# Layer 1 of a hybrid encoder: memory heads placed among the state-space units, the units' states in PSUM, and a wider filler rule for VectorE

## The chip, the core and the metric

The kernel runs on one core of a Trainium2 chip. The core has TensorE (PE: matmuls, with weight loads shown as PEld), VectorE (DVE), ScalarE (ACT), GpSimd (POOL) and SyncE (SP, which here issues every DMA). SBUF is the working memory, PSUM the eight banks of 512 float32 words a partition into which matmuls write; POOL works on SBUF alone here. The metric is the device time of one execution in microseconds (us).

## The reference, cut to what matters

Two post-norm layers over 512 tokens of width 1024, one batch. Layer 0 has a convolution branch, latent attention with 8 heads and attention of 4 heads into 256 memory tokens. Layer 1 has a bidirectional S5 state-space branch and another 4-head memory attention:

```python
def odd_layer(x, mem, w_in, s5_fwd, s5_bwd, s5_d, w_glu, w_mem_kv, w_out, ln_g, ln_b):
    h = x @ w_in
    s5_u, s5_gate, mem_q, mem_gate = _split(h, ODD_SPLITS)
    y = s5_direction(u, *s5_fwd, reverse=False) + s5_direction(u, *s5_bwd, reverse=True)
    y = y.reshape(bsz, seq, S5_DIM) + s5_d * s5_u
    z = jax.nn.gelu(y) @ w_glu
    c_out = (z[..., :S5_DIM] * jax.nn.sigmoid(z[..., S5_DIM:])) * jax.nn.silu(s5_gate)
    m_out = memory_attention(mem_q, mem, w_mem_kv) * jax.nn.silu(mem_gate)
    out = jnp.concatenate([c_out, m_out], axis=-1) @ w_out
    return layer_norm(ALPHA * x + out, ln_g, ln_b)
```

The memory heads need only `h` and the memory tokens; the state-space branch does not feed them. The gated products (`z @ w_glu`) need all 1024 channels of `z`, so every state-space unit must be done first.

## The kernel before

Every float32 product is made of three products of a rounded part and a remainder (`mm3`). So each weight that arrives by DMA is first copied to its rounded part by ScalarE (a CAST) and then has its remainder taken by VectorE (a TENSOR_TENSOR), both 128x1024; a projection of 128 output channels is then 24 matmuls of 512 columns. The loads go through `wload`; up to three raw weights are held.

The code does not issue instructions as it is written. It records them (`Prog.record`), and `Prog.schedule` then places all of them in one list by a simulation of its own with costs per instruction: an instruction is placed when its inputs are ready, its engine is free and its tiles can be had. SBUF and PSUM space is given out by tag; `QUOTA` says how many tiles of a tag may live at once. Instructions are taken by their recorded order (`prio`), up to a `WINDOW` of 500 recorded instructions ahead; background work (convolution taps, the state-space tables of `s5_prep`) fills gaps. Each engine then runs its part of that list in order, and waits by semaphores. The scheduler marks instructions with `port`: those of POOL, and those of VectorE that read two SBUF tensors. It takes them to exclude each other, and when VectorE would find the port taken it looks for one of its instructions that needs no port and ends soon enough (line 432).

Layer 1 is `layer1`. After the memory keys and values (`mem_kv`) come eight input projections `s5_u`, then eight units `s5_unit(i)`, each with the projection of one gate (`gate`) behind it, then the four memory heads (`mem_attn`), then eight gated products (`glu_out`, two projections each) and the output projection (`out_proj`), whose order is memory heads first.

A unit holds 128 channels. TensorE makes the input of the states (8 products of 256 columns, line 1314), transposes it (8 transposes, line 1325) into two PSUM banks Z, its real and imaginary part. VectorE then rotates by a table E: four products E*Z; two additions give Vr. Four scans of 64 partitions (forward on 64, backward on the others, for each part) give W, whose first or last column in each of 8 groups is then set to zero. Four products E*W and two additions give X, the states. TensorE multiplies X and the inputs with tables C and strips (24 products, line 1367), and after every second unit the result is transposed (line 1380), goes through GELU on ScalarE and becomes two of the eight z tiles. Seven loads of a unit come from tables that `s5_prep` wrote to device memory in layer 0.

A memory head is one gate projection, one projection of queries, scores in two banks (12 matmuls of 256 columns), a softmax with exponentials on ScalarE, 8 transposes and 6 matmuls with the values.

Of the kernel before, what the change touches and what calls it, by code (L numbers as in the profile page):

```python
# [14 lines left out]
F32 = mybir.dt.float32  # L15
# [3 lines left out]
ALU = mybir.AluOpType  # L19
# [4 lines left out]
P = 128  # L24
# [37 lines left out]

SB_WORDS = {"S": 21504, "R": 26624, "Z": 4864}
ENGINES = ("PE", "DVE", "ACT", "POOL", "SP")
QUOTA = dict(wr=3, wh=4, wl=4, wrv=1, whv=1, wlv=1, wrk=1, whk=1, wlk=1, A=4, S=3, T=2, R=1, Q=1, O=4, V=1, Z=2, W=2, Y=1, pr=6, bb=2, bt=2, nat=2, ncim=2, strips=2, qE=1, qt=2, qbt=1, qpw=1, qC=2, qB=1, C=2, D=1, cgl=2)
INF = float("inf")
NEAR, RESERVE = 30, dict(R=3584, S=2048)
RESERVEP = dict(R=4096, S=2560)
RESERVE1 = dict(R=2048, S=512)
WINDOW = dict(PE=500, DVE=500, ACT=700, POOL=500, SP=250)  # L70
# [109 lines left out]
class Prog:  # L180
# [108 lines left out]
    def schedule(self):  # L289
# [26 lines left out]
        order, left, t = [], len(self.ops), 0.0  # L316
# [86 lines left out]
        while left:  # L403
# [12 lines left out]
            t, e = max(t, best[0]), best[1]  # L416
# [7 lines left out]
            while pend[e] and pend[e][0][0] <= t:  # L424
                r, p, i, o = heapq.heappop(pend[e])
                heapq.heappush(avail[e], (p, i, o))
            skipped, got = [], None
            near = main[front].prio + NEAR if front < len(main) else INF
            if e == "DVE" and port > t + 80.0:

                for c in sorted(avail[e])[:40]:
                    if not c[2].port and c[2].cost < port - t + 150.0 and (c[2].bg or c[0] <= near - NEAR + WINDOW[e]) and alloc(c[2], near):
                        got = c[2]
                        avail[e].remove(c)
                        heapq.heapify(avail[e])
                        break
            while got is None and avail[e] and len(skipped) < 200:
                if not avail[e][0][2].bg and front < len(main) and avail[e][0][0] > main[front].prio + WINDOW[e]:

                    c = next((x for x in sorted(avail[e]) if x[2].bg), None)  # L440
# [4 lines left out]
                else:  # L445
                    c = heapq.heappop(avail[e])
# [91 lines left out]
class Kernel:  # L538
# [132 lines left out]
    def setup(self):  # L671
        nc, A = self.nc, self.A
        self.ident = self.ct([P, P], F32, "ident")
        self.ones = self.ct([P, P], F32, "ones")
        self.mhalf = self.ct([P, 8], F32, "mhalf")
        self.halfpi = self.ct([P, 1], F32, "halfpi")
        self.vec = self.ct([P, V_TOT], F32, "vec")
        nc.vector.memset(self.ones[:], 1.0)
        self.ones_r = self.ct([P, P], F32R, "onesr")
        nc.scalar.copy(self.ones_r[:], self.ones[:])  # L680
        nc.vector.memset(self.mhalf[:], -0.5)
        nc.vector.memset(self.halfpi[:], 1.5707963267948966)

        warm = self.bank("Y")
        for _ in range(8):
            nc.tensor.matmul(warm[:, 0:P], lhsT=self.ones[:], rhs=self.ones[:], start=True, stop=True)

        self.X = []

        W = [[nc.tile([P, 1024], dt, tag) for dt, tag in ((F32, "wr"), (F32R, "wh"), (F32R, "wl"))] for _ in range(2)]  # L690
        for step in ((0, 0, 256), 0, 1, (1, 0, 256), (0, 256, 1024), 2, 3, (1, 256, 1024), 4, 5, 6, 7):
            if isinstance(step, int):
                raw = self.big()
                nc.sync.dma_start(out=raw[:], in_=A["xT"][step // 2][:, (step % 2) * N:(step % 2 + 1) * N])
                self.X.append(self.split(raw[:]))
            else:
                c, sl = step[0], slice(*step[1:])
                raw, hi, lo = (t[:, sl] for t in W[c])
                nc.sync.dma_start(out=raw, in_=A["w1"][c][:, sl])
                self.split_into(raw, hi, lo)  # L700
        self.w0 = [w[1:] for w in W]
# [280 lines left out]
        V = [self.split(ps[:]) for ps in pv]  # L982
        return K, V

    def mem_attn(self, wq, wg, act, K, V):
        nc = self.nc
        scale = 128.0 ** -0.5
        out = []
        for h in range(4):
            g = self.gate(wg[h], act)  # L990
            ps = self.projF(wq[h], act, 8)
            qh, ql = self.split(ps[:])
            kh, kl = (x[:, (h % 2) * 256:(h % 2) * 256 + 256] for x in K[h // 2])
            pr = []
            for u in range(2):
                s = self.bank("S")
                for i in range(2):
                    t = 2 * u + i
                    self.mm3(s[:, i * 256:i * 256 + 256], [(qh[:, t * P:(t + 1) * P], ql[:, t * P:(t + 1) * P])],
                             [(kh, kl)])  # L1000
                mx = self.sm(2, tag="mx2")
                nc.vector.reduce_max(mx[:], s[:].rearrange("p (a b) -> p a b", a=2), axis=AX.X)
                p = self.big(F32, "pr")
                for i in range(2):
                    sl = slice(i * 256, i * 256 + 256)
                    self.softmax_tail(s[:, sl], p[:, sl], scale, mx[:, i:i + 1])
                pr.append(p)
            pt = []
            for m in range(2):
                tp = self.bank("T")  # L1010
                for t in range(4):
                    c = (t % 2) * 256 + m * P
                    nc.tensor.transpose(tp[:, t * P:(t + 1) * P], pr[t // 2][:, c:c + P], self.ident[:])
                pt.append(self.split(tp[:]))
            o = self.bank("V")
            vs = slice(h * P, h * P + P)
            self.mm3(o[:], [(v[0][:, vs], v[1][:, vs]) for v in V], [(a[:], b[:]) for a, b in pt])
            nc.vector.scalar_tensor_tensor(g[:], o[:], 0.5, g[:], op0=ALU.mult, op1=ALU.mult)
            out.append(g)
        return out  # L1020


    def out_proj(self, wname, mix, resid, grow, brow, finish, tail):
# [269 lines left out]
    def s5_unit(self, i):  # L1293
# [34 lines left out]
        nc.scalar.copy(dv, self.m8[:, i * 8:i * 8 + 8].unsqueeze(2).to_broadcast([P, 8, 64]))  # L1328
        G.memset(dv[0:64, :, 0:1], 0.0)
        G.memset(dv[64:128, :, 63:64], 0.0)  # L1330
        Vr = [self.big(), self.big()]
        t = [self.tmp() for _ in range(2)]
        V.tensor_tensor(Vr[0][:], E[0], Z[0][:], op=ALU.mult)
        V.tensor_tensor(t[0][:], E[1], Z[1][:], op=ALU.mult)
        V.tensor_tensor(Vr[1][:], E[0], Z[1][:], op=ALU.mult)
        V.tensor_tensor(t[1][:], E[1], Z[0][:], op=ALU.mult)
        G.tensor_tensor(Vr[0][:], Vr[0][:], t[0][:], op=ALU.add)
        G.tensor_tensor(Vr[1][:], Vr[1][:], t[1][:], op=ALU.subtract)
        W = [self.big(), self.big()]
        for x in range(2):  # L1340
            wv = W[x][:].rearrange("p (n k) -> p n k", n=8)
            V.tensor_tensor_scan(W[x][0:64, 1:N], D0[0:64, 0:N - 1], Vr[x][0:64, 0:N - 1], 0.0,
                                 op0=ALU.mult, op1=ALU.add)
            V.tensor_tensor_scan(W[x][64:128, 0:N - 1][:, ::-1], D0[64:128, 1:N][:, ::-1],
                                 Vr[x][64:128, 1:N][:, ::-1], 0.0, op0=ALU.mult, op1=ALU.add)
            G.memset(wv[0:64, :, 0:1], 0.0)
            G.memset(wv[64:128, :, 63:64], 0.0)
        X = [self.big(), self.big()]
        t = [self.tmp() for _ in range(2)]
        G.tensor_tensor(X[0][:], E[0], W[0][:], op=ALU.mult)  # L1350
        V.tensor_tensor(t[0][:], E[1], W[1][:], op=ALU.mult)
        G.tensor_tensor(X[1][:], E[0], W[1][:], op=ALU.mult)
        V.tensor_tensor(t[1][:], E[1], W[0][:], op=ALU.mult)
        G.tensor_tensor(X[0][:], X[0][:], t[0][:], op=ALU.subtract)
        G.tensor_tensor(X[1][:], X[1][:], t[1][:], op=ALU.add)
# [5 lines left out]
        for q in range(4):  # L1361
            c = q * P
# [67 lines left out]
    def layer0(self):  # L1430
# [11 lines left out]
        K, V = self.mem_kv("m0")  # L1442
        mq = A["w1"][40:44]
        mgt = A["w1"][44:48]
        mem = self.mem_attn(mq, mgt, self.xact, K, V)
        for c in range(4):
            nc.sync.dma_start(out=self.mixd[8 + c][:], in_=mem[c][:])
        self.rope_tables()
# [48 lines left out]
    def layer1(self):  # L1497
        nc, A = self.nc, self.A
        nc.res = RESERVE1
        act = lambda k: tuple(x[:, k % 4] for x in self.H[k // 4])  # L1500
        K, V = self.mem_kv("m1")
        self.z, self.sg = [None] * 8, [None] * 8
        for i in range(8):
            self.s5_u(i, act)
        for i in range(8):
            self.s5_unit(i)
            self.sg[i] = self.gate(A["w2"][8 + i], act)
        mem = self.mem_attn(A["w2"][16:20], A["w2"][20:24], act, K, V)
        mem = [self.split(m[:]) for m in mem]
        zact = lambda k: (self.z[k][0][:], self.z[k][1][:])  # L1510
        cs = [self.glu_out(c, zact) for c in range(8)]
        grow, brow = self.rows("o_ln_g", "o_ln_b")
        ov = self.out.rearrange("(k s) d -> s k d", s=SC)

        def finish(t, h):

            for half in range(2):
                for s in range(2):
                    nc.sync.dma_start(out=ov[2 * t + s, :, half * N:(half + 1) * N], in_=h[half][s * NCH:(s + 1) * NCH, :])

        def resid(t, half):
            r = self.tmp()
            nc.sync.dma_start(out=r[:], in_=self.h1d[t][half][:])
            return r

        self.out_proj("wo1", mem + cs, resid, grow, brow, finish, TAIL[1])
# [94 lines left out]
```

## Time and profile before

| | us |
|---|---|
| median of 3 runs | 1098.17 |
| lowest and highest | 1095.62, 1101.28 |
| profiled execution, its time | 1099.12 |
| its span, first to last instruction | 1097.3 |
| PE busy | 1016.5 (93%) |
| DVE busy | 805.2 (73%) |
| ACT busy | 440.9 (40%) |
| POOL busy | 558.5 (51%) |
| mean granted TensorE clock | 0.966 |

A share over the whole span is a mean over stages with different limits, so the stages are read one by one: the windows below give each engine's busy time in a stretch, the chain of waits says what each piece of the path waited for, and the groups by form give how long one instruction takes. All instructions carry one line number (535, where the list is emitted), so groups are told apart by engine, operation and tiles: `sb` and `sr` are the SBUF arenas, `sz` the one for small tiles, `ps` is PSUM, `scr` device memory, `w` the layers' input weights.

### The profile page before, as it was taken

The numbers are of one execution on the slowest core, as the hardware profiler recorded it, in microseconds if no ns is written. First come the engines' busy times: TensorE is split into PE (matmuls) and PEld (weight loads), VectorE is DVE, ScalarE is ACT, GpSimd is POOL, SyncE is SP. The second block draws the span as 40 slices with busy tenths as digits, with TensorE's granted clock in tenths as the row PEclk, the third lists the DMA queues.
The fourth block names the chain that finished last, engine by engine and source line by source line (L and its number), as shares of the span: only waits on it lengthen the run. The fifth ranks groups of instructions, "written<-read, shape, count | busy, mean of one in ns | idle before, by whom it ended". The sixth has DMA issues, their size and how long they took to land.

```text
span 1097.3 us, 15060 instructions
## 1 busy us (share of the span) xinstructions
PE 1016.5 (93%) x5296; PEld 797.7 (73%) x5296; DVE 805.2 (73%) x1252; ACT 440.9 (40%) x760; POOL 558.5 (51%) x805
## 2 busy tenths in 40 slices
PE   9999899999999979996889899997788799999996
PEld 7888678878777646764667688875556588888885
DVE  6787999999899888889885448419677946543346
ACT  5433356364323554566562224422222356422210
POOL 0554568758799687895989901006556600000001
PEclk9999999999999988998999899999899899999998
DMA  7434534335775262546396754984676422333413
GB/s 252 138 113 146 162 107 162 135 106 181 248 231 178 65 209 96 169 129 212 127 306 211 272 186 146 304 285 122 195 221 222 118 77 78 114 135 120 147 60 76
DMA packets 80171, 180.02 MB, mean 164 GB/s; under 512 B 24160, under 2 KB 28896, under 8 KB 80096
## 3 DMA queue, kind: packets, MB, share of 16 engines
q1 hardware_dynamic: 80096, 179.07, 50.2%
q8 instruction: 41, 0.67, 0.3%
q14 instruction: 34, 0.28, 0.1%
HBM read 142.93 MB, written 36.11 MB: 163 GB/s over the span
## 4 chain that ended last, share of the span: by engine, by line
PE 53%; DVE 11%; DMA 8%; POOL 7%; ACT 4%; issue 2%; SPq 1%; DVEq 0%; ACTq 0%; POOLq 0%
PE ps L535 53%; POOL sb L535 7%; DVE sr L535 4%; DMA sb<-w 4%; DVE ps L535 4%; DVE sb L535 2%; ACT sb L535 2%; ACT sr L535 2%; DMA scr<-sb 1%; DMA sb<-wo 1%; SPq L535 1%; DMA sb<-pos 1%; DVE sz L535 0%; DMA sb<-m1v 0%; POOL sz L535 0%
## 5 line engine op out<-in xcount | busy, mean ns | idle before, releaser
L535 PE MATMUL ps<-sr 128*128 128x512 f32 (+2 forms) x3904 | 933.4, 394 | 55.7 <-ACT sr L535 38.7
L535 PEld LDWEIGHTS ps<-sr 128*128 128x128 f32 (+1 forms) x3904 | 715.8, 192 | 229.8 <-ACT sr L535 45.2
L535 DVE TENSOR_TENSOR sr<-sb,sr 128x1024 fp32r<-128x1024 f32 (+4 forms) x230 | 274.4, 1203 | 165.6 <-ACT sr L535 142.1
L535 POOL TENSOR_TENSOR sb<-sb 128x512 f32<-128x512 f32 (+6 forms) x278 | 297.6, 1084 | 110.5 <-DVE sb L535 59.4
L535 ACT CAST sr<-sb 128x1024 fp32r<-128x1024 f32 (+4 forms) x230 | 201.1, 887 | 334.6 <-PE ps L535 180.8
L535 POOL TENSOR_TENSOR sz<-sz 128x64 f32<-128x64 f32 (+2 forms) x75 | 41.4, 556 | 252.9 <-DVE sz L535 252.8
L535 DVE SCALAR_TENSOR_TENSOR ps<-sb,sz,ps 128x505 f32<-128x505 f32 (+14 forms) x240 | 168.6, 736 | 0.3
L535 POOL TENSOR_TENSOR sb<-sb,sz 128x512 f32<-128x512 f32 (+4 forms) x160 | 132.3, 845 | 29.2 <-DVE sz L535 10.7
L535 ACT COPY sb<-ps 128x512 f32<-128x512 f32 (+3 forms) x78 | 41.0, 541 | 95.6 <-PE ps L535 74.2
L535 DVE SCALAR_TENSOR_TENSOR sb<-sb,ps 128x512 f32<-128x512 f32 x64 | 47.4, 740 | 42.1 <-ACT sb L535 22.9
L535 ACT CAST sr<-ps 128x512 fp32r<-128x512 f32 (+1 forms) x100 | 55.4, 571 | 52.7 <-PE ps L535 52.1
L535 DVE TENSOR_TENSOR sr<-ps,sr 128x512 fp32r<-128x512 f32 (+1 forms) x100 | 65.1, 661 | 12.4 <-ACT sr L535 10.2
L535 PE MATMUL ps<-sz,sb 128*128 128x128 f32 (+2 forms) x608 | 63.6, 238 | 8.7 <-ACT sb L535 5.6
L535 PEld LDWEIGHTS ps<-sz,sb 128*128 128x128 f32 (+1 forms) x608 | 46.9, 131 | 28.4 <-ACT sb L535 14.8
L535 PE MATMUL ps<-sb 128*64 128x128 f32 (+2 forms) x768 | 56.9, 302 | 6.2 <-POOL sb L535 2.4
L535 POOL TENSOR_TENSOR sb<-sz 64x64 f32<-64x64 f32 (+1 forms) x128 | 58.9, 469 | 4.8
L535 ACT ACTIVATE sb<-ps 128x512 f32<-128x512 f32 (+1 forms) x72 | 38.1, 548 | 51.2 <-PE ps L535 37.2
L535 PEld LDWEIGHTS ps<-sb 128*64 128x64 f32 (+1 forms) x768 | 35.6, 129 | 30.9 <-issue 18.8
L535 POOL MEMSET sb<- 64x8 f32 (+2 forms) x80 | 11.0, 148 | 89.0 <-DMA scr<-sb 34.8
L535 DVE TENSOR_TENSOR_SCAN sb<-sb 64x511 f32<-64x511 f32 x32 | 50.2, 1570 | 6.8 <-POOL sb L535 2.5
L535 ACT ACTIVATE sb<-ps,sz 128x256 f32<-128x256 f32 (+1 forms) x64 | 36.6, 578 | 36.4 <-DVE sz L535 31.3
L535 DVE TENSOR_REDUCE sz<-ps 128x1 f32<-128x512 f32 (+1 forms) x48 | 32.0, 684 | 14.2 <-PE ps L535 14.0
(45 smaller groups left out, 350.4 us busy)
## 6 DMA issues: line engine op xcount, KB each, us to landing
sb<-w SPq DMA_DIRECT2D x70, 512.0 KB
sb<-scr SPq DMA_DIRECT2D x48, 512.0 KB
scr<-sb SPq DMA_DIRECT2D x40, 512.0 KB
sb<-scr SPq DMA_DIRECT2D x76, 256.0 KB
sb<-wo SPq DMA_DIRECT2D x32, 512.0 KB
scr<-sb SPq DMA_DIRECT2D x46, 256.0 KB
sb<-s5bt SPq DMA_DIRECT2D x16, 512.0 KB
sb<-wglu SPq DMA_DIRECT2D x16, 512.0 KB
```

Of the source, the lines that this page charges most:

```text
L535: o.ins = getattr(eng[o.eng], o.meth)(*[real(x) for x in o.a], **{k: real(v) for k, v in o.k.items()})
```

## The change

Four things are edited.

The memory heads become a generator (`mem_heads`) that yields one head's gated result. In layer 0 it is run through at once, as before. In layer 1 a head is recorded after every second unit, and its split into rounded part and remainder with it.

In a unit, Vr takes two PSUM banks of a new tag U (quota 2) instead of SBUF tiles, and W is written over the two Z banks (`W = Z`). [...] The last two additions of X stay on POOL.

In the scheduler, when VectorE would find the port taken, it may take a port-free instruction that ends up to 300 ns after the port comes free, where it was 150.

One tile of zeros is set at the start.

```diff
-QUOTA = dict(wr=3, wh=4, wl=4, wrv=1, whv=1, wlv=1, wrk=1, whk=1, wlk=1, A=4, S=3, T=2, R=1, Q=1, O=4, V=1, Z=2, W=2, Y=1, pr=6, bb=2, bt=2, nat=2, ncim=2, strips=2, qE=1, qt=2, qbt=1, qpw=1, qC=2, qB=1, C=2, D=1, cgl=2)
+QUOTA = dict(wr=3, wh=4, wl=4, wrv=1, whv=1, wlv=1, wrk=1, whk=1, wlk=1, A=4, S=3, T=2, R=1, Q=1, O=4, V=1, Z=2, W=2, Y=1, pr=6, bb=2, bt=2, nat=2, ncim=2, strips=2, qE=1, qt=2, qbt=1, qpw=1, qC=2, qB=1, C=2, D=1, cgl=2, U=2)
...
-                    if not c[2].port and c[2].cost < port - t + 150.0 and (c[2].bg or c[0] <= near - NEAR + WINDOW[e]) and alloc(c[2], near):
+                    if not c[2].port and c[2].cost < port - t + 300.0 and (c[2].bg or c[0] <= near - NEAR + WINDOW[e]) and alloc(c[2], near):
...
+        self.zeros = self.ct([P, 8], F32, "zeros")
+        nc.vector.memset(self.zeros[:], 0.0)
...
-    def mem_attn(self, wq, wg, act, K, V):
+    def mem_heads(self, wq, wg, act, K, V):
...
-            out.append(g)
-        return out
+            yield g
...
-        Vr = [self.big(), self.big()]
+        Vr = [self.bank("U"), self.bank("U")]
         t = [self.tmp() for _ in range(2)]
         V.tensor_tensor(Vr[0][:], E[0], Z[0][:], op=ALU.mult)
         V.tensor_tensor(t[0][:], E[1], Z[1][:], op=ALU.mult)
+        V.tensor_tensor(Vr[0][:], t[0][:], Vr[0][:], op=ALU.add)
+        V.tensor_tensor(t[1][:], E[1], Z[0][:], op=ALU.mult)
         V.tensor_tensor(Vr[1][:], E[0], Z[1][:], op=ALU.mult)
-        V.tensor_tensor(t[1][:], E[1], Z[0][:], op=ALU.mult)
-        G.tensor_tensor(Vr[0][:], Vr[0][:], t[0][:], op=ALU.add)
-        G.tensor_tensor(Vr[1][:], Vr[1][:], t[1][:], op=ALU.subtract)
-        W = [self.big(), self.big()]
+        V.tensor_tensor(Vr[1][:], Vr[1][:], t[1][:], op=ALU.subtract)
+        W = Z
         for x in range(2):
...
-            G.memset(wv[0:64, :, 0:1], 0.0)
-            G.memset(wv[64:128, :, 63:64], 0.0)
+            nc.scalar.copy(wv[0:64, :, 0:1], self.zeros[0:64].unsqueeze(2))
+            nc.scalar.copy(wv[64:128, :, 63:64], self.zeros[64:128].unsqueeze(2))
         X = [self.big(), self.big()]
         t = [self.tmp() for _ in range(2)]
-        G.tensor_tensor(X[0][:], E[0], W[0][:], op=ALU.mult)
+        V.tensor_tensor(X[0][:], E[0], W[0][:], op=ALU.mult)
         V.tensor_tensor(t[0][:], E[1], W[1][:], op=ALU.mult)
-        G.tensor_tensor(X[1][:], E[0], W[1][:], op=ALU.mult)
+        V.tensor_tensor(X[1][:], E[0], W[1][:], op=ALU.mult)
...
+        heads = self.mem_heads(A["w2"][16:20], A["w2"][20:24], act, K, V)
+        mem = []
         for i in range(8):
             self.s5_unit(i)
             self.sg[i] = self.gate(A["w2"][8 + i], act)
-        mem = self.mem_attn(A["w2"][16:20], A["w2"][20:24], act, K, V)
-        mem = [self.split(m[:]) for m in mem]
+            if i % 2:
+                mem.append(self.split(next(heads)[:]))
```

What this does to the order in which engines get their instructions is shown at three places. First VectorE in the fourth unit of layer 1 (index 3), before: four scans (64x511), the gate's product, two X products from SBUF, then the next unit's products E*Z.

```order
L535 TENSOR_TENSOR sb<-sb,ps 128x512 x2
L535 SCALAR_TENSOR_TENSOR sb<-sb 64x511 x4
L535 SCALAR_TENSOR_TENSOR sb<-sb,ps 128x512
L535 TENSOR_TENSOR sb<-sb 128x512 x2
L535 TENSOR_TENSOR sb<-sb,ps 128x512 x2
L535 TENSOR_TENSOR sr<-sb,sr 128x1024
L535 TENSOR_TENSOR sb<-sb,ps 128x512 x2
```

The same unit on VectorE now, from its first product to the remainder of the gate's weights behind it.

```order
L535 TENSOR_TENSOR ps<-sb,ps 128x512
L535 TENSOR_TENSOR sr<-sb,sr 128x512
L535 TENSOR_TENSOR sb<-sb,ps 128x512 x2
L535 TENSOR_TENSOR ps<-sb,ps 128x512 x2
L535 SCALAR_TENSOR_TENSOR ps<-sb,ps 64x511
L535 TENSOR_TENSOR ps<-ps,sb 128x512
L535 SCALAR_TENSOR_TENSOR ps<-sb,ps 64x511 x3
L535 TENSOR_TENSOR sb<-sb,ps 128x512 x4
L535 TENSOR_TENSOR sr<-sb,sr 128x1024
```

The additions stand between the products, scans and products all have a PSUM operand, and the unit runs to its last product before the next unit's first.

Second, TensorE behind the last unit, before: its last products (64x128), the gate, the transposes of z, then head 0's scores (128x256) between projections; three more heads follow.

```order
L535 MATMUL ps<-sb 64x128 x20
L535 MATMUL ps<-sr 128x512 x4
L535 MATMUL ps<-sz,sb 128x128 x8
L535 MATMUL ps<-sr 128x512 x29
L535 MATMUL ps<-sr 128x256 x2
L535 MATMUL ps<-sr 128x512 x4
L535 MATMUL ps<-sr 128x256 x10
L535 MATMUL ps<-sr 128x512 x18
L535 MATMUL ps<-sz,sb 128x128 x2
L535 MATMUL ps<-sr 128x512
```

TensorE at the same place now; the scores are those of head 3, the only head left.

```order
L535 MATMUL ps<-sb 64x128 x20
L535 MATMUL ps<-sr 128x512 x4
L535 MATMUL ps<-sz,sb 128x128 x8
L535 MATMUL ps<-sr 128x512 x44
L535 MATMUL ps<-sr 128x256 x2
L535 MATMUL ps<-sr 128x512 x7
L535 MATMUL ps<-sr 128x256 x10
L535 MATMUL ps<-sr 128x512 x21
L535 MATMUL ps<-sz,sb 128x128 x4
```

Of the 44 matmuls, 7 end the gate, 32 are head 3's two projections and 5 begin the gated products, which start behind three heads fewer.

Third, ScalarE in the seventh unit (index 6), now; before, no zeros stood here.

```order
L535 COPY ps<-sz 64x8
L535 COPY sb<-ps 128x512
L535 CAST sr<-ps 128x512
L535 COPY ps<-sz 64x8
L535 CAST sr<-ps 128x512
L535 COPY ps<-sz 64x8
L535 CAST sr<-sb 128x1024
L535 COPY sb<-ps 128x512
L535 COPY ps<-sz 64x8
```

The four zero copies (64x8) of the unit stand between copies of another unit's input, the casts of a head's probabilities and the cast of a gate's weights (128x1024). ScalarE's order now has 15 table loads, where it had 9.

## Rows read from the trace of the kernel before

**Rows 1.** The page's first line.
```profile
span 1097.3 us, 15060 instructions
```

**Rows 2.** Windows: length, busy time (instructions) of each engine, granted clock, DMA share, GB/s.
```profile
300.00:500.00 200.00, 186.62 (x999) 133.79 (x997) 179.06 (x291) 98.70 (x189) 174.15 (x219) 0.95 0.47 151
500.00:610.00 110.00, 90.02 (x490) 66.84 (x491) 83.71 (x122) 55.00 (x98) 93.73 (x111) 0.94 0.68 231
...
738.00:882.00 144.00, 116.85 (x828) 83.83 (x823) 112.18 (x103) 38.30 (x73) 79.66 (x86) 0.91 0.59 181
882.00:947.00 65.00, 64.99 (x320) 52.71 (x319) 37.30 (x76) 36.80 (x85) 0.00 (x0) 1.00 0.24 83
947.00:1088.00 141.00, 141.00 (x624) 116.59 (x622) 62.46 (x79) 32.85 (x39) 2.96 (x3) 1.00 0.33 105
```

**Rows 3.** Chain that ended last, 735 to 1098: start, length, what.
```profile
759.29 7.16 DMA sb<-w
...
814.26 9.54 DMA sb<-w
...
869.84 4.77 DMA sb<-w
...
894.64 193.59 PE ps L535 x880
```

**Rows 4.** Waits, 738 to 882: who on whom, us, times, longest.
```profile
PE ps L535 <- ACT sr L535: 23.6, 7, 6.3
ACT sr L535 <- DMA sb<-w: 22.8, 8, 5.5
```

**Rows 5.** VectorE by form, 738 to 947: busy us, mean ns, idle before.
```profile
L535 DVE TENSOR_TENSOR_SCAN sb<-sb 64x511 f32<-64x511 f32 x32 | 50.2, 1570 | 6.8 <-POOL sb L535 2.5 <-ACT sb L535 2.0 <-PE ps L535 1.7
...
L535 DVE TENSOR_TENSOR sb<-sb,ps 128x512 f32<-128x512 f32 x32 | 20.7, 679 | 13.4 <-PE ps L535 11.9 <-POOL sb L535 1.4
L535 DVE TENSOR_TENSOR sb<-sb 128x512 f32<-128x512 f32 x16 | 18.3, 1156 | 0.2
L535 DVE TENSOR_TENSOR sr<-sb,sr 128x512 fp32r<-128x512 f32 x12 | 8.2, 689 | 9.8 <-ACT sr L535 9.8
...
L535 DVE RECIPROCAL sz<-sz 128x1 f32<-128x1 f32 x16 | 2.5, 162 | 8.2 <-ACT sb L535 8.2
```

**Rows 6.** VectorE on sb, 738 to 947: ns min/median/max, first and last start.
```profile
L535 DVE TENSOR_TENSOR sb<-sb,ps x32: 654/679/689, 741.7 to 857.9; 128x512 f32<-128x512 f32 x32
L535 DVE TENSOR_TENSOR_SCAN sb<-sb x32: 1205/1220/2292, 744.4 to 865.9; 64x511 f32<-64x511 f32 x32
```

**Rows 7.** VectorE by form, 480 to 600: an addition in PSUM.
```profile
L535 DVE TENSOR_TENSOR ps<-sb,ps 128x512 f32<-128x512 f32 x7 | 4.8, 684 | 0.0
```

**Rows 8.** VectorE by form, 882 to 947: remainders of weights.
```profile
L535 DVE TENSOR_TENSOR sr<-sb,sr 128x1024 fp32r<-128x1024 f32 x10 | 12.1, 1220 | 1.7 <-ACT sr L535 1.3 <-PE ps L535 0.4
```

**Rows 9.** Windows, first to last vector work of the units.
```profile
741.00:872.00 131.00, 104.76 (x731) 74.97 (x730) 106.29 (x100) 33.36 (x63) 76.68 (x85) 0.90 0.59 178
```

**Rows 10.** POOL by form, 738 to 882.
```profile
L535 POOL TENSOR_TENSOR sb<-sb 128x512 f32<-128x512 f32 x48 | 76.4, 1606 | 70.1 <-DVE sb L535 57.6 <-PE ps L535 4.1 <-ACT sb L535 3.9
```

**Rows 11.** Timeline of TensorE behind the last unit: start, us, what.
```profile
877.16 2.40 PE L535 MATMUL ps<-sb 128*64 128x128 f32 x40
...
880.53 1.03 PE L535 MATMUL ps<-sz,sb 128*128 128x128 f32 x8
```

**Rows 12.** ScalarE by form, 738 to 947.
```profile
L535 ACT COPY sb<-ps 128x256 f32<-128x256 f32 x16 | 5.2, 376 | 46.7 <-PE ps L535 46.7
...
L535 ACT ACT_TABLE_LOAD x2 | 2.6, 1283 | 3.8 <-DVE sz L535 3.7
```

**Rows 13.** Timeline of TensorE in layer 0, with the idle time before each.
```profile
514.53 4.20 PE L535 MATMUL ps<-sr 128*128 128x512 f32 x8 [7.57 <-ACT sr L535]
...
609.03 3.35 PE L535 MATMUL ps<-sr 128*128 128x512 f32 x7 [4.69 <-ACT sr L535]
```

**Rows 14.** Timeline of SyncE's queue, 590 to 612.
```profile
590.75 0.32 SPq L535 DMA_DIRECT2D scr<-sz  x1
598.04 0.34 SPq L535 DMA_DIRECT2D scr<-sb  x1
...
601.25 1.61 SPq L535 DMA_DIRECT2D sb<-wo  x3
```

More of the change, by code (lines that the diff above doesn't have):

```diff
@@ L983, in mem_kv @@
         return K, V
-    def mem_attn(self, wq, wg, act, K, V):
+    def mem_heads(self, wq, wg, act, K, V):
         nc = self.nc
         scale = 128.0 ** -0.5
-        out = []
         for h in range(4):
@@ L1444, in layer0 @@
         mgt = A["w1"][44:48]
-        mem = self.mem_attn(mq, mgt, self.xact, K, V)
+        mem = list(self.mem_heads(mq, mgt, self.xact, K, V))
         for c in range(4):
```

## The prediction, made before the changed kernel was timed

> **What bounds the kernel now.** The span is 1097.3 us [rows 1]. I read the windows by stage first. Layer 1 has three parts: eight state-space units (738 to 882), four memory heads (882 to 947), then gated products and output projection. Behind 882 TensorE is busy all the time at full clock [rows 2]: 624 matmuls in 141.0 us, 0.226 us each. [...] From 894.64 on the chain is TensorE alone [rows 3]. So nothing but the units' stretch, and the stalls of layer 0 below, can give time.
>
> What is there: TensorE does 116.85 x 0.91 + 65 = 171 us of full-clock work between 738 and 947, which takes 209. At most 38 us can go in layer 1.
>
> **The change, part by part.**
>
> *Heads among the units.* No instruction is added on TensorE. In its order a whole head (48 matmuls of 512 columns and the small ones, some 15 us) now stands between the second unit of a pair and the next pair; behind the last unit only one head is left instead of four. That head work is what runs while a unit's vector chain is under way. It also gives weights time: I counted, in the list that schedule() returns, the matmul work placed between the issue of a gate's weights and their first use, at 0.226 us a matmul. For the gates of units 2 to 7 it is 1.7 to 7.8 us before and 9.5 to 14.3 after; the six weights of heads 0 to 2 have 4.2 to 23.7, head 3's two 3.8 and 5.3. Against DMAs of 5 to 9.5 us most of the 23.6 us of waiting goes. The scheduler's tiles allow the earlier issue because four 512-word tiles of each unit have left SBUF. What is late next is VectorE.
>
> *States in PSUM, and what VectorE takes over.* Per unit POOL loses four tensor operations and four memsets; VectorE gains four tensor operations; ScalarE gains four 64x8 copies of zeros. VectorE's list from the first unit's first product to the last unit's last X product grows from 99 to 183 instructions, since three heads now lie within it. Priced from rows:
> - 32 products E*Z and 32 X products, all with a PSUM source now, and 10 + 3 scalar_tensor_tensor of that shape: 77 x 0.679 = 52.3 us [rows 5]
> - 32 scans. Before they take 1.570 us in the mean and 1.205 at the fastest [rows 5, 6]; the shape is the same, and the difference is waiting behind POOL for the port that both use. With a PSUM source and output that wait goes. No row has a scan on PSUM: bounds 1.205 and 1.570. I take the median, 1.220, since other forms cost no more with PSUM (next line): 39.0 us; the upper bound would add 11.2.
> - 16 additions in PSUM at 0.684, a row of that form [rows 7]: 10.9 us
> - 10 remainders of weights at 1.220, as behind the units where POOL rests [rows 8]; in the units stage they waited too. 12.2 us
> - 18 remainders of half that size at 0.689 [rows 5], 6 reductions at about that: 16.5 us
> - 24 small ones at 0.162 at most [rows 5]: 3.9 us
>
> Sum 134.8 us. Before, the 99 instructions were busy 106.29 of the 131 us from 741 to 872, 81% [rows 9]. The waits behind POOL that go (32 x 0.35 us of scans, 16 x 0.47 of X products at 1.156 [rows 5]) pay for most of the 32 added operations.
>
> [...] The 0.684 us with a PSUM source stand beside 0.689 with SBUF sources [rows 5, 7], so this trace shows no surcharge. [...]
>
> A unit now holds its two Z banks and two U banks until its X products are done, so the next unit's transposes, and its first product, wait for that. VectorE's order shows one unit whole, then the next: a serial chain, with VectorE its only worker. At 100% the last X product ends at 741.7 + 134.8 = 876.5 (first start from [rows 6]; before: 871.6). It won't be 100%: between units VectorE waits for transposes, within one for ScalarE's zeros. In layer 0, where it has a store of background work, it is busy 179.06 of 200 us and 83.71 of 110, 90% and 76% [rows 2]. I take 87%: 155 us, the last X product at 896.6.
>
> From there: POOL's last addition about 2 us (1.6 [rows 10] and a hand-over), the unit's products 2.4 and transposes 1.0 [rows 11], 43 matmuls that stand ahead of the gated products (11 of the gate, 32 of head 3) 9.7, the first gated product with head 3's rest 10.8 + 3.8, then what follows 947 today, 141.0, and the 9.3 from 1088 to the end: 180 us. 896.6 + 180 = 1076.6, against 1097.3: 20.7 us less.
>
> *ScalarE.* 32 zero copies (no such row; between nothing and the 0.376 of a 128x256 copy [rows 12], at most 12 us) and six more table loads of 1.283 [rows 12], because exponentials and GELU now alternate: 7.7 us. ScalarE is busy 38.30 of 144 us there [rows 2], so I cost them at nothing; when VectorE's next instruction waits for one, it counts in the 87%.
>
> *The filler.* VectorE, when POOL holds the port, may now take a lock-free instruction that ends up to 300 instead of 150 ns late. This reorders layer 0. Between 500 and 610 TensorE idles 20 us [rows 2]; two pieces are plain: 7.57 us before 514.53 and 4.69 before 609.03 [rows 13]. The second is SyncE's queue: it waits until 598.04 for POOL's table work, with the weights of the second output half behind it [rows 14]. In the new order these weights stand some 9 us of matmul work earlier, and POOL's tables end about 6 earlier. I take 3 us of gain, from 10 down to a loss of 8 (one more such stall).
>
> Sum: 1097.3 - 20.7 - 3 = 1073.6. The profiled run took 1099.12, 1.8 beside its span: 1075.4. The median of the runs is 0.95 below that run: 1074.
>
> **Rivals.**
> - *TensorE bound.* The waits vanish and VectorE runs at 97 to 100%: last X at 877 to 881, end 1057 to 1061, by the clock sum 1059, less 3: about 1056. For it: head work everywhere. Against: one serial chain with hand-overs to two engines.
> - *VectorE no better used than elsewhere.* At 77% the last X is at 917 and the gain is gone: 1094 to 1098. For it: 76% in 500 to 610. Against: 81% today although it waits for POOL and DMAs.
> - *ScalarE passes DMA waits into the chain: slower.* The zero copies now stand among casts of weights on ScalarE; POOL's memsets did not. A cast that waits for its DMA holds the zeros, the zeros the X products, these the banks of the next unit. Price: 2.85 us a wait [rows 4], 14 weights: 40 us on top of the forecast, 1114. It decides from 29 us, ten such waits. Against it: the longer leads. [...]
> - *The filler hurts layer 0* by 8 to 10 us, layer 1 as forecast: 1087. That it does nothing gives 1077.
>
> **How the numbers follow.** Forecast 0.57 (VectorE at 80 to 95%: 1060 to 1088), TensorE bound 0.12, filler hurts 0.07, VectorE at 77% 0.13, ScalarE 0.11. The bound at the upper scan price (11 us) lies in the forecast's own range. From 1052 to 1100 leaves out the ScalarE case and a strip at either end. About 0.5% can be told from no change, 1092.7 to 1103.7. Faster: 0.57 + 0.12 + 0.07 = 0.76; same 0.11 and slower 0.02 of the third case; slower with ScalarE 0.13.
>
> **What would show it.** Right: waits of TensorE for casts in the units well under 10 us, VectorE over 85% busy there, scans of 1.2 us, the last X product near 897 less what layer 0 gives, one head behind it. Wrong: scans or additions on PSUM over 1.4 us; VectorE waiting for ScalarE's zeros more than 10 us; ScalarE still 20 us on weights; the gated products beginning after 930; or the first layer-1 product on VectorE later than 745.

## The result and the profile after

The changed kernel took 1064.57 us in the median of four executions, beside 1098.7 for the kernel before on the same chip. Three of them took 1060.0 to 1065.56 us; the fourth was slow, 5556.46 us at full clock, nothing here explains it, and it is left out of the ratio: 0.9674, 95% interval 0.9645 to 0.9704. The forecast was 1074, the range 1052 to 1100. The profiled execution took 1060.0; its page begins:

```profile
span 1058.2 us, 15020 instructions
## 1 busy us (share of the span) xinstructions
PE 1007.6 (95%) x5296; PEld 792.2 (75%) x5296; DVE 799.2 (76%) x1285; ACT 450.1 (43%) x798; POOL 514.7 (49%) x741
```

The span is 39.1 us shorter than in [rows 1]. To find where, I read two places off TensorE's timeline, counting matmuls in the kernel's order: the start of layer 1's eight input projections (before 694.0, after 675.2), and the time from their end (737.6, 718.9) to the start of the second gated product (946.6, 907.5). Layer 0 with its keys and values gave 18.7 us, layer 1 gave 20.4 (209.0 to 188.6); what follows takes the same. The windows after, with the columns of [rows 2]; the last is VectorE's stretch from the first E*Z product to the last X product:

```profile
300.00:500.00 200.00, 187.84 (x1032) 134.34 (x1032) 181.28 (x295) 105.89 (x205) 180.84 (x222) 0.98 0.53 170
500.00:610.00 110.00, 101.92 (x531) 77.72 (x531) 80.50 (x102) 50.66 (x84) 95.95 (x103) 0.93 0.70 227
719.00:884.00 165.00, 153.51 (x1034) 115.34 (x1033) 130.07 (x186) 72.01 (x165) 23.32 (x24) 0.97 0.55 173
884.00:908.00 24.00, 24.00 (x115) 19.56 (x114) 14.56 (x24) 15.54 (x31) 0.00 (x0) 1.00 0.41 140
908.00:1049.00 141.00, 141.00 (x623) 116.51 (x621) 63.04 (x80) 33.12 (x40) 2.96 (x3) 1.00 0.33 105
722.90:873.70 150.80, 139.97 (x942) 104.84 (x940) 126.30 (x184) 68.48 (x158) 20.90 (x23) 0.99 0.58 184
```

From 719 to 884, the units with three of the heads, TensorE now idles 11.5 of 165 us (27.2 of 144 before), at a granted clock of 0.97 instead of 0.91. Some of the waits from 719 to 884 (who on whom: us, times, longest):

```profile
ACT ps L535 <- DVE ps L535: 19.6, 15, 2.6
...
PE ps L535 <- POOL sb L535: 7.0, 4, 5.6
ACT sr L535 <- DMA sb<-w: 6.6, 2, 3.6
...
DVE ps L535 <- ACT ps L535: 1.1, 4, 0.4
```

TensorE's 23.6 us for casts and ScalarE's 22.8 for weights [rows 4] have become nothing in the list and 6.6. TensorE's largest wait is now the 7.0 us for POOL's last additions, 5.6 of it once. VectorE waits 1.1 us for ScalarE's zeros; it is ScalarE that waits for the scans. VectorE by form, 722.9 to 873.7:

```profile
L535 DVE TENSOR_TENSOR_SCAN ps<-sb,ps 64x511 f32<-64x511 f32 x32 | 39.2, 1224 | 1.8 <-ACT ps L535 1.1
L535 DVE TENSOR_TENSOR sb<-sb,ps 128x512 f32<-128x512 f32 x48 | 30.5, 680 | 0.3
L535 DVE TENSOR_TENSOR ps<-sb,ps 128x512 f32<-128x512 f32 x24 | 16.1, 690 | 4.5 <-issue 2.2 <-PE ps L535 2.2
L535 DVE TENSOR_TENSOR sr<-sb,sr 128x1024 fp32r<-128x1024 f32 x11 | 14.8, 1357 | 2.2 <-ACT sr L535 2.2
...
L535 DVE TENSOR_TENSOR ps<-ps,sb 128x512 f32<-128x512 f32 x8 | 5.3, 666 | 0.0
```

Scans take 1.224, the 48 products that write SBUF 0.680, half of the additions 0.666; the 24 at 0.690 are the other 16 products and 8 additions. The remainders of weights read two SBUF tensors and take 1.357, where [rows 8] had 1.220 with POOL at rest. Behind the last X product the chain of waits is, from 875.05 on, TensorE alone (start, length):

```profile
872.50 1.19 DVE sb L535 x2
873.70 1.31 DVE sr L535
...
875.05 174.04 PE ps L535 x794
```

### The profile page after: what moved, and what is told of

Same layout as the page of the kernel before. It is cut to its first block, busy times and chain, and to the rows that moved or that the text cites. A ratio compares the mean times of both kernels' runs of the same rounds, so it can differ in the third digit from the quotient of the medians.

```text
span 1058.2 us, 15020 instructions
## 1 busy us (share of the span) xinstructions
PE 1007.6 (95%) x5296; PEld 792.2 (75%) x5296; DVE 799.2 (76%) x1285; ACT 450.1 (43%) x798; POOL 514.7 (49%) x741
## 5 line engine op out<-in xcount | busy, mean ns | idle before, releaser
L535 PE MATMUL ps<-sr 128*128 128x512 f32 (+1 forms) x3904 | 925.5, 392 | 28.4 <-DVE sr L535 13.0
L535 PEld LDWEIGHTS ps<-sr 128*128 128x128 f32 x3904 | 709.9, 190 | 201.3 <-issue 21.7
L535 DVE TENSOR_TENSOR sr<-sb,sr 128x1024 fp32r<-128x1024 f32 (+4 forms) x230 | 270.1, 1186 | 172.4 <-ACT sr L535 130.2
L535 POOL TENSOR_TENSOR sb<-sb 128x512 f32<-128x512 f32 (+3 forms) x246 | 256.2, 1055 | 190.9 <-DVE sb L535 177.7
L535 DVE SCALAR_TENSOR_TENSOR ps<-sb,sz,ps 128x503 f32<-128x503 f32 (+14 forms) x240 | 167.5, 736 | 0.0
L535 POOL TENSOR_TENSOR sz<-sz 128x64 f32<-128x64 f32 (+2 forms) x75 | 44.4, 596 | 221.6 <-DVE sz L535 218.2
L535 POOL TENSOR_TENSOR sb<-sz 64x64 f32<-64x64 f32 (+1 forms) x128 | 55.3, 440 | 4.9
L535 DVE TENSOR_TENSOR sb<-sb,ps 128x512 f32<-128x512 f32 x63 | 40.4, 680 | 2.0 <-PE ps L535 1.3
L535 DVE TENSOR_TENSOR_SCAN ps<-sb,ps 64x511 f32<-64x511 f32 x32 | 39.2, 1224 | 1.8 <-ACT ps L535 1.1
L535 ACT ACTIVATE sb<-sb,sz 128x512 f32<-128x512 f32 (+1 forms) x65 | 38.2, 622 | 5.3 <-DVE sz L535 5.2
```

Of the source, the lines that this page charges most:

```text
L535: o.ins = getattr(eng[o.eng], o.meth)(*[real(x) for x in o.a], **{k: real(v) for k, v in o.k.items()})
```

## The experiments

"Start" is the start of layer 1's projections, "layer 1" the time from their end to the second gated product, both from the profiled execution; each ratio, with its interval, is to the kernel before as timed on the same chip with that run (medians of 1098.0 to 1100.3).

| run | time | ratio | start | layer 1 |
|---|---|---|---|---|
| before | 1098.7 | | 694.0 | 209.0 |
| after | 1064.6 | 0.967 (0.965 to 0.970) | 675.2 | 188.6 |
| filler_only | 1083.7 | 0.986 (0.980 to 0.991) | 680.6 | 206.9 |
| no_filler | 1079.9 | 0.982 (0.977 to 0.987) | 696.2 | 186.6 |
| heads_only | 1091.2 | 0.991 (0.988 to 0.994) | 695.4 | 200.4 |
| psum_only | 1098.1 | 0.998 (0.996 to 1.001) | 693.6 | 210.1 |
| heads_vector | 1079.5 | 0.982 (0.977 to 0.987) | 692.3 | 190.6 |
| space_held | 1059.2 | 0.967 (0.962 to 0.971) | 678.2 | 184.1 |
| pool_busy | 1062.5 | 0.965 (0.960 to 0.970) | 680.5 | 183.1 |
| heads_all | 1065.0 | 0.968 (0.963 to 0.973) | 674.3 | see below |
| filler_200 | 1064.6 | 0.967 (0.963 to 0.971) | 681.1 | 188.5 |
| filler_250 | 1077.0 | 0.982 (0.978 to 0.987) | 692.7 | 188.8 |
| filler_310 | 1083.0 | 0.988 (0.983 to 0.992) | 697.3 | 187.5 |
| filler_600 | 1145.5 | 1.044 (1.039 to 1.050) | 760.0 | 192.4 |

### The change taken apart

**filler_only**: the kernel before, one line.

```diff
-... c[2].cost < port - t + 150.0 and ...
+... c[2].cost < port - t + 300.0 and ...
```

> The kernel before with one edit: the filler rule allows 300 ns instead of 150. Theory A (layer 0's 18.7 us come from this rule, since VectorE fills more of its waits for the port): the layer-1 projections of the state-space branch start at about 675 us instead of 694, layer 1 is as before, and the time is 1080 (1076 to 1084). Rival B (the gain is an accident of a list that changed elsewhere): their start stays at 690 to 698 and the time at 1094 to 1102.

**no_filler**: the changed kernel with that line back.

> The changed kernel with the rule back at 150 ns. Theory A: layer 0 is that of the kernel before (projections of layer 1 start at 694), layer 1 keeps its 20 us: 1078 to 1084. Rival B: 1062 to 1068, the projections at about 675.

Both came out as Theory A said: the filler line alone moves the start (to 680.6, not all the way to 675), the rest alone gives layer 1. In all five kernels with 150 here (before, no_filler, heads_only, psum_only, heads_vector) layer 0's instructions stand in the same order but for one memset; their starts are 692.3 to 696.2, in the mean 694.3. The same holds of five with 300 (after, filler_only, space_held, pool_busy, heads_all): 674.3 to 680.6, mean 677.8. So the line is worth 16.5 us in layer 0, and a single profile is uncertain by about 3. What in the line gives it, the sweep below asks.

**heads_only**: `mem_heads` and the new loop in `layer1`, nothing else. **psum_only**: the new `s5_unit`, the tag U and the tile of zeros, nothing else.

> The kernel before with one edit: a memory head recorded after every second unit; states in SBUF, rule at 150 ns. Theory C (the work of the heads beside the units' vector chains, and the longer lead of weights, is the whole of layer 1's gain; VectorE gets about 25 us of head work and 106 us of its own, near the 135 us of the changed kernel): 1076 to 1082. Rival D (without the states in PSUM the added work on VectorE and its waits for the port make the chain late): 1088 to 1100.

> The kernel before with one edit: the units' states in PSUM, with the additions and products on VectorE and the zeros on ScalarE; heads behind the units, rule at 150 ns. Theory C: scans at 1.22 us, VectorE's work per unit about the same, weights as late as before, so 1094 to 1102. Rival D: the chain of a unit gets shorter by 3 us or more and layer 1 gains 10 us or more: 1080 to 1089.

PSUM alone gave nothing that can be told, as Theory C said, though its scans took 1.225 us. Heads alone took 1091.2, in the bounds of Rival D, and gave 8.6 us in layer 1, not the 16 to 22 of Theory C: it falls. Alone the two parts give 8.6 and -1.1, together 22.4 (no_filler). VectorE's stretch, first E*Z to last X product, shows why; psum_only, then heads_only:

```profile
741.30:869.10 127.80, 105.43 (x720) 75.09 (x718) 103.60 (x131) 38.31 (x95) 23.06 (x21) 0.89 0.61 187
```

```profile
744.20:910.80 166.60, 148.87 (x945) 109.76 (x944) 127.88 (x152) 64.16 (x126) 79.28 (x87) 0.95 0.54 166
```

Without heads TensorE has too little to do in the units (105 us, clock 0.89), and the heads' 65 us stay behind them. VectorE's stretch is 2.1 us shorter than before (129.9), and even this is lost behind it, where the last unit's 40 products take 3.70 us in psum_only and 2.40 before [rows 11], behind a wait of 3.48 us for POOL. With heads it is the units' vector work that the rest waits for: heads_only needs 127.88 us busy for 152 instructions where the changed kernel does 184 in 126.30, and its stretch is 15.8 us longer, 14.2 of them idle time of VectorE (38.7 against 24.5 us).

### What heads alone lacked: space in SBUF, PSUM, or POOL out of the way

**space_held**: the changed kernel, with the SBUF space of Vr and W taken again.

```diff
+        held = [self.big() for _ in range(4)]
+        for x in held:
+            G.tensor_copy(x[0:1, 0:1], t[0][0:1, 0:1])
...
+        for x in held[:2]:
+            G.tensor_copy(x[0:1, 0:1], X[0][0:1, 0:1])
+        for x in held[2:]:
+            G.tensor_copy(x[0:1, 0:1], X[1][0:1, 0:1])
```

> The changed kernel, but each unit holds four extra tiles of 512 words in SBUF from its first E*Z product to its X products, as the kernel before did for Vr and W; nothing reads them (POOL writes one word into each at either end). Theory S (heads alone gained 8.6 us in layer 1 and heads with PSUM 22.4 because PSUM frees the space that weights need to be loaded early): layer 1 falls back to about 200 us from the end of the last input projection to the second gated product, 1074 to 1080. Rival P (it is VectorE's chain, which no longer waits for POOL and its port): it stays at 187 to 191 us, 1062 to 1068.

184.1 us: Theory S falls, the space is not it. (From the third unit on its order differs from the changed kernel's, so its few us less than Rival P's 187 to 191 are not read as a gain.)

**heads_vector**: heads_only, with four operations handed from POOL to VectorE and the states left in SBUF.

```diff
-        G.tensor_tensor(Vr[0][:], Vr[0][:], t[0][:], op=ALU.add)
-        G.tensor_tensor(Vr[1][:], Vr[1][:], t[1][:], op=ALU.subtract)
+        V.tensor_tensor(Vr[0][:], Vr[0][:], t[0][:], op=ALU.add)
+        V.tensor_tensor(Vr[1][:], Vr[1][:], t[1][:], op=ALU.subtract)
...
-        G.tensor_tensor(X[0][:], E[0], W[0][:], op=ALU.mult)
+        V.tensor_tensor(X[0][:], E[0], W[0][:], op=ALU.mult)
...
-        G.tensor_tensor(X[1][:], E[0], W[1][:], op=ALU.mult)
+        V.tensor_tensor(X[1][:], E[0], W[1][:], op=ALU.mult)
```

> The kernel with only the heads moved (states in SBUF, rule at 150 ns), and the two additions of Vr and the two X products that POOL made are now VectorE's, still on SBUF tiles. Theory P (what heads alone lacked is that POOL stands in the unit's chain, by hand-overs and by holding the port; PSUM is only one way to get it out): layer 1 takes 186 to 191 us from the end of the last input projection to the second gated product, 1078 to 1083. Rival Q (the states must be in PSUM, since VectorE on two SBUF operands still meets POOL's last additions at the port and the tiles still fill SBUF): 197 us or more, 1088 or more.

190.6 us and 1079.5: Theory P, in the middle of its bounds, and the time of no_filler (1079.9) without one state in PSUM. What heads alone lacked is POOL out of the unit's chain, but for the two last additions of X, which POOL makes in every run. Only one list with heads has POOL's products in the chain (200.4 us); the lists without them (heads_vector, space_held, pool_busy, and that of the changed kernel and its filler runs), which order much of layer 1 differently, lie at 183.1 to 192.4. The scans in SBUF, heads_only and then heads_vector:

```profile
L535 DVE TENSOR_TENSOR_SCAN sb<-sb 64x511 f32<-64x511 f32 x32 | 50.1, 1566 | 1.5 <-POOL sb L535 0.9
```

```profile
L535 DVE TENSOR_TENSOR_SCAN sb<-sb 64x511 f32<-64x511 f32 x32 | 38.8, 1214 | 0.7
```

**pool_busy**: the changed kernel, with four more products on POOL in each unit.

```diff
+        d = [self.big(), self.big()]
+        for x in range(4):
+            G.tensor_tensor(d[x % 2][:], E[x // 2], t[x % 2][:], op=ALU.mult)
         W = Z
```

> The changed kernel with four more products of 128x512 on POOL in each unit, from the E*Z products' tiles, so that POOL holds the port while VectorE scans; nothing reads them. Theory P in its port form (a VectorE instruction with one operand in PSUM does not wait for POOL): scans stay at 1.22 us and products at 0.68, layer 1 at 184 to 192 us, 1058 to 1068. Rival R (scans in PSUM wait too; they were short only since POOL rested): scans in the mean over 1.4 us, layer 1 over 195 us, 1072 or more.

Theory P's port form holds: scans in PSUM take 1.225 us although POOL works beside them, and layer 1 takes 183.1 us, 0.9 under its bounds. A piece of the timeline, VectorE and then POOL:

```profile
730.95 1.21 DVE L535 TENSOR_TENSOR_SCAN ps<-sb,ps 64x511 f32<-64x511 f32 x1
...
732.78 3.75 DVE L535 TENSOR_TENSOR_SCAN ps<-sb,ps 64x511 f32<-64x511 f32 x3
```

```profile
729.47 5.00 POOL L535 TENSOR_TENSOR sb<-sb 128x512 f32<-128x512 f32 x4 [45.72 <-DVE sb L535]
```

I counted which of the 32 scans overlap a POOL product in time. In heads_only 21 do: 1.750 us in the mean, the other 11 1.215. In pool_busy 21 do: 1.221, the other 11 1.231. So in these two traces a scan beside a POOL product takes longer when it reads and writes SBUF alone (`sb<-sb`), and no longer when it reads and writes PSUM as well (`ps<-sb,ps`). A wait for the port means this lengthening; of the port itself the traces show no more.

What stays open is how the 10 to 14 us of layer 1 between heads_only and the two kernels without POOL in the chain (heads_vector, no_filler) divide: VectorE's waits for the port (32 scans by 0.35, 16 X products by 0.30 above 0.684: 16 us busy) and the hand-overs to POOL and back. No run separated them. VectorE's busy time is the same in heads_only and heads_vector (127.88 and 127.49 us), since the 32 operations taken over fill what the port gave back; what shrank is its idle time, from 38.7 to 26.0 us.

**heads_all**: the changed kernel with the fourth head earlier.

```diff
-            if i % 2:
+            if i in (1, 3, 5, 6):
```

> The changed kernel with the heads recorded after units 1, 3, 5 and 6 (counted from 0) instead of 1, 3, 5 and 7: no head stands behind the last unit. Theory T (TensorE has some 10 us of idle time left in the units' stretch, and VectorE gets about 8 us more work there): the units end 5 to 10 us later, what follows is 15 us shorter, 1054 to 1061. Rival U (the head pushes the last unit's chain back by as much as it fills): 1063 to 1072.

1065.0, Rival U. Part of the second gated product now comes earlier, so layer 1 is measured to the end of the output projection: 333.5 us, 330.2 in the changed kernel. From the last input projection to the last unit's end:

```profile
718.00:898.00 180.00, 168.45 (x1109) 126.50 (x1108) 143.20 (x208) 83.51 (x187) 22.76 (x24) 0.99 0.54 171
```

TensorE idles 180 - 168.45 = 11.55 us here, as it did in the 165 us of the changed kernel (11.49). The head filled no gap; the stretch grew by its length.

### Is it the rule, or this one list?

**filler_200, filler_250, filler_310, filler_600**: the changed kernel with another number.

```diff
-... c[2].cost < port - t + 300.0 and ...
+... c[2].cost < port - t + 310.0 and ...
```

> The changed kernel with 200 ns in the filler rule. Theory L (each value gives another list for layer 0, and what it is worth can't be read from the value: 150 gave a start of layer 1's projections at 694 to 696, 250 at 693, 300 at 675 to 681, 310 at 697, 600 at 760): any start from 672 to 700, 1060 to 1086. Rival A (a trend with a jump between 250 and 300): start at 690 to 697, 1076 to 1083.

> The changed kernel with 250 ns in the filler rule instead of 300. Theory A (what layer 0 gains follows from how much of VectorE's waiting for the port may be filled): between 150 and 300 the time falls steadily, so layer 1's projections start between 675 and 685 and the time is 1064 to 1072. Rival L (the rule shuffles a long list; a gain or loss of some 5 us is chance on top of it): any start between 668 and 690, also before 675; 1058 to 1078.

> The changed kernel with 310 ns in the filler rule instead of 300: few instructions have a length that only this admits. Theory A: projections start at 673 to 677, time 1062 to 1067. Rival L: a different list, and the start moves by 5 us or more to either side, so 1070 or more, or 1060 or less.

> The changed kernel with 600 ns in the filler rule: any port-free instruction of up to 0.6 us beyond the wait may go ahead. Theory A, taken further (more filling is better): 1060 or less. Rival H (work pulled ahead makes what VectorE owes to TensorE late, so there is a best value in between): layer 0 longer than with 300, projections after 685, 1075 or more.

Starts at 150, 200, 250, 300, 310 and 600 ns: 694, 681, 693, 678, 697, 760 (means of five profiles each at 150 and 300). The view called L holds, though filler_250 starts 2.7 us beyond its bounds there, and Theory A falls: there is no trend from 150 to 310. The list's own simulation starts these projections at 640, 633, 632, 635, 646 and 700 us: it sees 310 and 600 as late, but ranks 250 ahead of 300, where the chip has it 15 us behind. From 300 to 310 VectorE's order in layer 0 is the same for 222 instructions, then one tap goes ahead, and by the list that schedule() returns some 600 of the 959 places then hold another instruction. Layer 0 in one window, after and then filler_310:

```profile
0.00:675.00 675.00, 644.98 (x3335) 504.59 (x3336) 574.88 (x976) 314.73 (x545) 487.19 (x711) 0.98 0.54 177
```

```profile
0.00:675.00 675.00, 630.30 (x3199) 490.02 (x3200) 551.13 (x954) 305.86 (x531) 477.40 (x706) 0.97 0.52 170
```

TensorE's waits from 0 to 690 (to 675 after), after and then filler_310:

```profile
PE ps L535 <- DVE sr L535: 14.4, 13, 2.6
...
PE ps L535 <- ACT sr L535: 3.0, 7, 0.6
```

```profile
PE ps L535 <- DVE sr L535: 22.5, 18, 3.6
...
PE ps L535 <- ACT sr L535: 3.4, 7, 0.7
```

With 310 ns the remainders that TensorE waits for (sr) come later 18 times instead of 13, and VectorE is busy 24 us less in these 675 us. Why that list is worse than its neighbour I can't say from a rule; it differs nearly everywhere. At 600 the direction is Rival H's; 100 to 300 us, filler_600:

```profile
100.00:300.00 200.00, 125.54 (x686) 99.61 (x684) 193.09 (x325) 57.76 (x111) 171.73 (x308) 0.80 0.41 136
```

```profile
PE ps L535 <- POOL sb L535: 56.9, 7, 23.3
PE ps L535 <- DVE sr L535: 15.3, 5, 8.8
```

VectorE is busy 193.09 of 200 us, as in the changed kernel (192.80), but with 186 convolution taps where that had 145 and 24 remainders of weights (`sr<-sb,sr`) where that had 45. TensorE stands 15.3 us for remainders and 56.9 for POOL's results, 23.3 of it once before a transpose, and is busy 125.54 of 200 us, where it was 193.99. So a busy VectorE did other work than what TensorE needed next; how far VectorE made POOL's results late, and how far the new order of TensorE and POOL did, no run shows.

No run beats the changed kernel by more than the intervals: space_held, pool_busy, filler_200 and heads_all overlap it.

## Why the prediction was right, and where it was wrong

*What bounds the kernel*: right. TensorE waited for late weights: 23.6 us for casts, while ScalarE waited 22.8 for weights [rows 4], with DMAs of 4.77 to 9.54 us in the chain [rows 3]. With head work between the units the waits went (6.6 us of ScalarE's were left) and the granted clock rose from 0.91 to 0.97. Idle time fell by 15.7 us, and what the lower clock cost, as an estimate, from 10.5 (116.85 by 0.09) to 4.6 (153.51 by 0.03): 21.6 together, against the 20.4 by which layer 1 got shorter.

*VectorE's price*: right. The prices summed to 134.8 us; the own durations of the 183 instructions that it priced sum to 136.7 (the 184th of the window, a remainder, begins at its end). The scan, 1.220 taken between 1.205 and 1.570, took 1.224.

*The share of 87%*: the size came right by two slips. A window counts overlapping instructions once, so the stretch is 126.30 of 150.80, 84%, under the 85% that I named as a sign; but my sum counts them each, and 136.7 of 150.8 is 91%. I had set a sum against shares from windows (81%, 90%, 76%), two measures that differ by 8% here. The stretch took 150.8 us, 155 forecast.

*Behind the last X product*: 180 forecast, 184.5 measured (873.7 to 1058.2). The sum took the products and the gate's matmuls at full clock. But TensorE had just stood 5.63 us for POOL, and what came next ran at a granted clock of 0.50 (875.05 to 877.55) and 0.56 (the 40 products, in the window below). These took 4.19 us where [rows 11] has 2.40 at a granted clock of 1.00, the five gate matmuls ahead of them 2.50 us where five at 0.226 make 1.13: 3.2 of the 4.5. Two rows of the timeline and the window of the 40 products:

```profile
873.97 0.69 PE L535 MATMUL ps<-sb 128*64 128x128 f32 x4 [5.63 <-POOL sb L535]
875.05 2.50 PE L535 MATMUL ps<-sr 128*128 128x512 f32 x5 [0.39 <-DVE sr L535]
```

```profile
877.48:881.67 4.19, 4.19 (x42) 4.02 (x41) 0.00 (x0) 0.00 (x0) 0.00 (x0) 0.56 0.01 4
```

The 4.2 gained ahead and the 4.5 lost here cancel, which is luck; layer 1's 20.4 beside 20.7 is better than its parts.

*ScalarE at nothing*: right, 1.1 us of VectorE's time for zeros. The slower rival fell with the waits for weights, of which 6.6 us were left.

*The filler*: the mis-sized term. "I take 3 us of gain, from 10 down to a loss of 8" stands against 18.7 in the profile, 16.5 over five profiles. I had looked at two stalls between 500 and 610 only. One of them, 7.57 us before 514.53 [rows 13], is 3.38 after and the other is gone, but the gain was there by 450: the fourth latent head's last matmul came at 431.9 instead of 452.1. The bounds failed too, since another number in the same rule gives anything from 17 us of gain to 66 of loss. With 18.7 in place of 3 the sum would have been 1057.9 us of span, against 1058.2.

*Rivals*: "TensorE bound" came near the time (1056), but not by its mechanism: VectorE did not run at 97 to 100%, and 16 of its us are the filler's. heads_all shows that the fourth head among the units gains nothing more.

*PSUM*: the prediction took what comes with PSUM for one thing. The runs part it: POOL leaving the chain is worth 10 us of layer 1 with heads there (heads_vector) and, with PSUM, nothing without (psum_only). PSUM itself shows nothing in the time (1079.9 beside 1079.5); in layer 1 it may be worth the other 2 to 4 us (186.6 to 188.8 in five profiles with 150 to 310 ns, 190.6 in the one of heads_vector).

## What to carry to other kernels

Two edits can be worth more together than their sum (8.6 and -1.1 us alone, 22.4 together), when the first puts work beside a chain that the second shortens; so take a change apart both ways before calling a part useless. A number in a greedy scheduler is a seed as much as a rule: time its neighbours (here 10 ns more cost 18 us) before explaining what it does, and bound such a term by their spread, not by the stalls that one can see. Set a sum of instruction durations only against a share that was measured the same way.

## What the runs showed of the hardware that was not expected

The overlap costs both sides. POOL's 128x512 operations took 1.35 us in the mean where they overlapped a scan in PSUM (22 in pool_busy; four in 5.00 us above), but 1.83 where they overlapped one in SBUF (15 in heads_only, the shortest 1.27). One of these:

```profile
806.99 2.03 POOL L535 TENSOR_TENSOR sb<-sb 128x512 f32<-128x512 f32 x1
```

Scans that read and write PSUM took 0.010 us more than scans in SBUF that met no POOL operation (1.224, and 1.214 in heads_vector), and X products 0.004 less (0.680 beside 0.684, the median in heads_vector). ScalarE's 64x8 zeros into PSUM, for which the prediction had no row, took 0.163 us each, 5.2 for 32.
